# Row normalization streamed through four buffers: from tiles of 12 rows to tiles of 13, 13, 13 and 12 rows

## The chip, the cores and the metric

The kernel runs on one core of a Trainium2 chip. The metric is the device time of one execution in microseconds (us), given as the median of five runs. The profiled execution is one further run, recorded by the hardware profiler.

## The reference

```python
# x: (32, 512, 1024) float32
sums = np.sum(np.abs(x), axis=-1, keepdims=True)
return (x / (sums + 1e-8)).astype(np.float32)
```

Each of the 32 x 512 = 16384 rows of 1024 numbers is divided by the sum of its absolute values. The input is 67.11 MB, and the output is as large.

## The kernel before

The 16384 rows are spread over 128 partitions, so each partition handles 128 rows of 4 KiB. They go through in tiles. A tile holds `R = 12` rows for each partition, 48 KiB a partition and 6.29 MB in all; ten such tiles and one of 8 rows make up the 128 (`rows`, L31 to L33). In memory each tile is one contiguous block, of which partition p owns the p-th run of 12 rows (`piece`, L35 to L37).

The buffers come from one pool with `BUFS = 4` buffers of 12 rows (L39): 192 KiB a partition. Small pools of four buffers hold the sums `s` and their reciprocals `inv` (L40).

The loop over the tiles (L70) issues for each tile, in this order:

- L72, from SyncE's queue (SP): the load of the tile. Before the fifth tile and each later one SP waits until the store of the tile four places earlier has landed, since both use the same buffer.
- L45, VectorE (DVE): one reduce that gives the sum of absolute values for every row of the tile; L52 adds the epsilon, L54 takes the reciprocal.
- L55, VectorE: multiplies the first `kv = k // 2` rows of the tile by their reciprocals, in place.
- L62, ScalarE (ACT): multiplies the other `k - kv` rows, one activation for each row, in place. It runs beside L55.
- L74, from ScalarE's queue: the store of the tile. It waits for L55 and for the last activation.

The order of each queue is the order in which the loop writes its instructions (`manual_schedule`); nothing reorders them. GpSimd (POOL) only sets four constants at the start, and TensorE isn't used. Loads and stores therefore lie in two queues, q1 (issued by SP) and q10 (issued by ACT), which are served by the same 16 DMA engines.

Of the kernel before, what the change touches and what calls it, by code (L numbers as in the profile page):

```python
# [1 line left out]

# [4 lines left out]

FP32 = mybir.dt.float32
EPS = 1e-8


@with_exitstack
def kernel(
    ctx: ExitStack,
    tc: tile.TileContext,
    x: bass.AP,
    out: bass.AP,
):
    nc = tc.nc
    P = nc.NUM_PARTITIONS  # L20

    x_flat = x.flatten_outer_dims()
    out_flat = out.flatten_outer_dims()
    n, d = x_flat.shape


    R = 12
    BUFS = 4
    per_partition = n // P
    assert n % P == 0  # L30
    rows = [R] * (per_partition // R)  # L31
    if per_partition % R:
        rows.append(per_partition % R)  # L33

    def piece(flat, i):  # L35
        a, k = P * sum(rows[:i]), rows[i]
        return flat[a : a + P * k, :].rearrange("(p r) d -> p r d", p=P)  # L37

    sbuf = ctx.enter_context(tc.tile_pool(name="sbuf", bufs=BUFS))  # L39
    stats = ctx.enter_context(tc.tile_pool(name="stats", bufs=4))  # L40

    def normalize(x_tile, r0, k, kv):

        s = stats.tile([P, R], FP32)
        nc.vector.tensor_reduce(  # L45
            out=s[:, :k],
            in_=x_tile[:, r0 : r0 + k, :],
            axis=mybir.AxisListType.X,
            op=mybir.AluOpType.add,
            apply_absolute_value=True,  # L50
        )
        nc.vector.tensor_scalar_add(out=s[:, :k], in0=s[:, :k], scalar1=EPS)  # L52
        inv = stats.tile([P, R], FP32)
        nc.vector.reciprocal(out=inv[:, :k], in_=s[:, :k])  # L54
        nc.vector.tensor_mul(  # L55
            out=x_tile[:, r0 : r0 + kv, :],
            in0=x_tile[:, r0 : r0 + kv, :],
            in1=inv[:, :kv].unsqueeze(2).to_broadcast([P, kv, d]),
        )
        for r in range(kv, k):  # L60
            row = x_tile[:, r0 + r, :]
            nc.scalar.activation(  # L62
                out=row,
                in_=row,
                func=mybir.ActivationFunctionType.Copy,
                scale=inv[:, r : r + 1],
            )

    with tc.manual_schedule():
        for i, k in enumerate(rows):  # L70
            x_tile = sbuf.tile([P, R, d], FP32)
            nc.sync.dma_start(out=x_tile[:, :k, :], in_=piece(x_flat, i))  # L72
            normalize(x_tile, 0, k, k // 2)
            nc.scalar.dma_start(out=piece(out_flat, i), in_=x_tile[:, :k, :])  # L74


# [1 line left out]
_INS = ['x']  # L78
_OUTS = [((32, 512, 1024), 'float32')]


# [23 lines left out]
```

## Time and profile before

| what | value |
|---|---|
| median of five runs | 317.55 us (317.2 to 318.51) |
| profiled execution, time | 317.17 us |
| profiled execution, span from first to last instruction | 315.5 us |
| bytes moved by DMA | 134.23 MB, mean 425 GB/s over the span |
| reduce L45, 12 rows | 12.95 us each |
| reduce L45, 8 rows | 8.69 us |
| multiply L55, 6 rows | 6.56 us each |
| activation L62, one row | 1.13 us each in the page's mean; six in a row take 6.34 us |
| load L72, median from issue to landing | 38.6 us |
| store L74, median from issue to landing | 53.3 us |

The span is cut by the profiler at the first and the last instruction; 1.67 us of the execution's time lie around it. Busy times are sums over an engine's instructions and leave out the issuing of DMAs. "Landing" is the moment at which the semaphore of a DMA has its full count, and the time to it includes waiting in the queue behind earlier transfers. In the windows view each row is one stretch of the span, with its length, the busy time and instruction count of VectorE, ScalarE and GpSimd, the clock column, the mean busy share of the 16 DMA engines and the rate in GB/s.

### The profile page before, as it was taken

Reading aid. Unit: us, or ns where it says so; the run is one execution under the profiler, and the core shown is the slowest. Engines: PE = TensorE matmul, PEld = TensorE weight load, DVE = VectorE, ACT = ScalarE, POOL = GpSimd, SP = SyncE. Lnnn points to the kernel's source line nnn. Section 1 sums busy time; section 2 is a strip of 40 time slices with the busy share of each in tenths; the row PEclk is TensorE's granted clock in tenths of the full one; section 3 lists DMA queues with packets and bytes.
Section 4 is the critical chain, followed back from the end, with each engine's and each line's share of the span. In section 5 each row is a group of like instructions: output and inputs, shape, how many; then the busy total and the mean of one; then the engine's idle time right before and its main releaser. Section 6 shows DMA issues by size and latency. Waiting matters only on the chain.

```text
span 315.5 us, 227 instructions
## 1 busy us (share of the span) xinstructions
DVE 212.4 (67%) x44; ACT 69.0 (22%) x65; POOL 0.2 (0%) x4
## 2 busy tenths in 40 slices
DVE  0069999999499079719944991797099449949300
ACT  0010804308007000700440070007003400611300
POOL 0000000000000000000000000000000000000000
DMA  8999999999999999999999999999999999999996
GB/s 318 467 411 436 449 349 449 411 461 424 411 474 417 405 480 417 411 474 411 424 461 411 425 461 411 442 442 411 461 430 405 467 411 453 422 455 417 417 438 274
DMA packets 3169, 134.23 MB, mean 425 GB/s; under 512 B 352, under 2 KB 352, under 8 KB 352
## 3 DMA queue, kind: packets, MB, share of 16 engines
q1 hardware_dynamic: 1584, 67.11, 49.8%
q10 hardware_dynamic: 1584, 67.11, 49.1%
q14 instruction: 1, 0.01, 0.0%
HBM read 67.11 MB, written 67.11 MB: 425 GB/s over the span
## 4 chain that ended last, share of the span: by engine, by line
another core or an unknown queue 45%; DMA 30%; DVE 17%; SPq 1%; issue 0%; DVEq 0%; ACTq 0%
DMA x_tile<-in_x_dram 16%; DMA out_dram<-x_tile 14%; DVE s L45 11%; DVE x_tile L55 6%; SPq L72 1%; DVE inv L54 0%; DVE s L52 0%; DVEq L54 0%; ACTq L74 0%
## 5 line engine op out<-in xcount | busy, mean ns | idle before, releaser
L45 DVE TENSOR_REDUCE s<-x_tile 128x12 f32<-128x12288 f32 (+1 forms) x11 | 138.2, 12564 | 80.9 <-DMA x_tile<-in_x_dram 80.9
L62 ACT ACTIVATE x_tile<-x_tile,inv 128x1024 f32<-128x1024 f32 x64 | 67.7, 1135 | 207.4 <-DVE inv L54 207.4
L55 DVE TENSOR_TENSOR x_tile<-x_tile,inv 128x6144 f32<-128x6144 f32 (+1 forms) x11 | 70.0, 6364 | 0.4
L62 ACT ACT_TABLE_LOAD x1 | 1.3, 1283 | 18.4 <-DMA x_tile<-in_x_dram 18.4
L54 DVE RECIPROCAL inv<-s 128x12 f32<-128x12 f32 (+1 forms) x11 | 2.5, 225 | 0.9
L52 DVE TENSOR_SCALAR s<-s 128x12 f32<-128x12 f32 (+1 forms) x11 | 1.9, 173 | 0.4
L89 POOL MEMSET const-bfloat16-1.0<- 128x1 bf16 x1 | 0.1, 102 | 0.0
L89 POOL MEMSET const-uint8-127<- 128x1 uint8 x1 | 0.1, 101 | 0.0
L89 POOL MEMSET const-float32-0.0<- 128x1 f32 x1 | 0.1, 99 | 0.2 <-issue 0.2
L89 POOL MEMSET const-float32-1.0<- 128x1 f32 x1 | 0.1, 98 | 0.0
## 6 DMA issues: line engine op xcount, KB each, us to landing
x_tile<-in_x_dram SPq DMA_DIRECT2D x10, 6144.0 KB, 38.6
out_dram<-x_tile ACTq DMA_DIRECT2D x10, 6144.0 KB, 53.3
x_tile<-in_x_dram SPq DMA_DIRECT2D x1, 4096.0 KB, 33.8
out_dram<-x_tile ACTq DMA_DIRECT2D x1, 4096.0 KB, 19.5
```

The lines of the kernel that those rows point to most:

```text
L45: nc.vector.tensor_reduce(out=s[:, :k], in_=x_tile[:, r0 : r0 + k, :], axis=mybir.AxisListType.X, op=mybir.AluOpType.add, apply_absolute_v ...
L52: nc.vector.tensor_scalar_add(out=s[:, :k], in0=s[:, :k], scalar1=EPS)
L54: nc.vector.reciprocal(out=inv[:, :k], in_=s[:, :k])
L55: nc.vector.tensor_mul(out=x_tile[:, r0 : r0 + kv, :], in0=x_tile[:, r0 : r0 + kv, :], in1=inv[:, :kv].unsqueeze(2).to_broadcast([P, kv, d]),)
L62: nc.scalar.activation(out=row, in_=row, func=mybir.ActivationFunctionType.Copy, scale=inv[:, r : r + 1],)
L72: nc.sync.dma_start(out=x_tile[:, :k, :], in_=piece(x_flat, i))
L89: nc = _bacc.Bacc("TRN2", target_bir_lowering=False, num_devices=1)
```

## The change

The tile size becomes 13 rows, except in the fourth buffer, which has 12. The single pool of four equal buffers is replaced by four pools of one buffer each: 13 + 13 + 13 + 12 = 51 rows, 204 KiB a partition. The list of tiles becomes 13, 13, 13, 12, 13, 13, 13, 12, 13, 13: ten tiles for eleven.

The mapping of tiles to memory changes as well. Four tiles in a row, which fill all buffers once, form a group. The group is one contiguous block of 128 x 51 rows, of which each partition owns 51 rows in a row; tile 0 of the group takes the first 13 rows of each partition's 51, tile 1 the next 13, and so on. Within a tile a partition's 13 rows are contiguous (52 KiB), but the runs of neighbouring partitions lie 51 rows (204 KiB) apart. The third group has two tiles, 26 rows a partition.

The arithmetic, the split between VectorE (`k // 2` rows) and ScalarE (the rest) and the order of the loop stay as they are. A tile of 13 rows gives VectorE 6 rows and ScalarE 7.

```diff
-    R = 12
-    BUFS = 4
-    per_partition = n // P
+    R = 13
+    SLOTS = [R, R, R, R - 1]
     assert n % P == 0
-    rows = [R] * (per_partition // R)
-    if per_partition % R:
-        rows.append(per_partition % R)
+    left = n // P
+    rows = []
+    while left:
+        rows.append(min(left, SLOTS[len(rows) % len(SLOTS)]))
+        left -= rows[-1]
 
     def piece(flat, i):
-        a, k = P * sum(rows[:i]), rows[i]
-        return flat[a : a + P * k, :].rearrange("(p r) d -> p r d", p=P)
+        g = i - i % len(SLOTS)
+        group = rows[g : g + len(SLOTS)]
+        a, m = P * sum(rows[:g]), sum(group)
+        b = sum(rows[g:i])
+        whole = flat[a : a + P * m, :].rearrange("(p r) d -> p r d", p=P)
+        return whole[:, b : b + rows[i], :]
 
-    sbuf = ctx.enter_context(tc.tile_pool(name="sbuf", bufs=BUFS))
+    slots = [
+        ctx.enter_context(tc.tile_pool(name=f"slot{b}", bufs=1))
+        for b in range(len(SLOTS))
+    ]
...
         for i, k in enumerate(rows):
-            x_tile = sbuf.tile([P, R, d], FP32)
+            x_tile = slots[i % len(SLOTS)].tile([P, SLOTS[i % len(SLOTS)], d], FP32)
```

## The prediction

> **What bounds the kernel now.** I read the page's busy times first, then the DMA rows, then the chain of waits, the windows and the timeline.
>
> ```profile
> DVE 212.4 (67%) x44; ACT 69.0 (22%) x65; POOL 0.2 (0%) x4
> ...
> DMA  8999999999999999999999999999999999999996
> ```
> No engine is busy throughout: VectorE works two thirds of the span. The DMA row is at 9 in all slices but the first and the last, so transfers are the suspect.
>
> ```profile
> q1 hardware_dynamic: 1584, 67.11, 49.8%
> q10 hardware_dynamic: 1584, 67.11, 49.1%
> ```
> Loads (q1) and stores (q10) together take 98.9% of the time of the 16 DMA engines. 1584 packets over 11 tiles are 144 a tile: 128, one for each partition, and 16 small ones (of the 3169 packets 352, or 16 for each of the 22 DMAs, are under 512 B). So a partition's 12 rows, 48 KiB, go as one packet.
>
> ```profile
> 102.43 0.33 SPq L72
> 102.76 0.05 issue
> 102.81 0.02 SPq L72
> 102.83 28.48 another core or an unknown queue
> 131.31 0.02 issue
> 131.32 0.03 SPq L72
> 131.35 0.03 issue
> 131.38 0.33 SPq L72
> 131.71 28.64 another core or an unknown queue
> ```
> The chain runs through the loads of L72, 29.0 us apart (102.43, 131.38). Between two of them SP waits until a store has landed and so freed a buffer. In one period a tile is read and a tile is written: 2 x 6.291 MB in 29.0 us is 434 GB/s.
>
> ```profile
> 0.00:1.00 1.00, 0.00 (x0) 0.00 (x0) 0.20 (x4) 1.00 0.00 0
> 1.00:18.30 17.30, 0.00 (x0) 0.00 (x0) 0.00 (x0) 1.00 0.99 409
> 18.30:40.00 21.70, 21.55 (x5) 7.62 (x7) 0.00 (x0) 1.00 1.01 435
> 102.00:131.00 29.00, 19.83 (x5) 6.27 (x7) 0.00 (x0) 1.00 1.00 434
> ...
> 281.00:295.00 14.00, 13.48 (x4) 4.27 (x4) 0.00 (x0) 1.00 1.02 442
> 295.00:314.50 19.50, 0.00 (x0) 0.00 (x0) 0.00 (x0) 1.00 0.88 381
> ```
> The last two columns are DMA share and GB/s. The rate is the same with loads alone (18.3 to 40, 435), both (434) and stores alone (281 to 295, 442). The DMA engines themselves are the bound, and what goes through them doesn't matter. 134.22 MB at 434 GB/s are 309.3 us of the span's 315.5; the other **6.2 us** lie at the two ends (nothing before 1.0, 409 until 18.3, 381 at the end).
>
> **The change, part by part.** The reference point is the profiled execution: span 315.5, time 317.17, so 1.67 us lie around the span. The median of the five runs is 317.55, 0.38 above it.
>
> *Bytes.* The same 134.22 MB: 0.
>
> *Fewer DMAs.* 10 tiles (13, 13, 13, 12, 13, 13, 13, 12, 13, 13) for 11, so 20 DMAs for 22, 16 x 20 small packets for 352. They cost only what the DMA engines lose at a border between DMAs. From below nothing. From above: 102 to 131 holds one border of each queue, 18.3 to 40 one of a single queue, and the rates differ by under 1%, so at most 0.3 us for two borders. Between them I take the trace's single packets, which the views only sum up: one of 48 KiB takes 1.815 us, one of 32 KiB 1.213 us. That is 37.6 ns for each KiB and 9 ns fixed. Each engine moves 8 packets a DMA, so 2 x 8 x 9 ns = 0.14 us are saved in the packets; with something for the two borders, whose bound was 0.3, I take **-0.2 us**. The Trainium skill, "DMA: Bandwidth & Descriptors", section "Anatomy of one DMA", gives a DMA about 2 us of fixed cost (for the GpSimd path); were it on the path here, two fewer would give -4 us, but the window of 29 us, with two DMA ends and no loss in it, says that it is covered.
>
> *Larger pieces on the engines.* A reduce of 13 rows takes 12.95 + (12.95 - 8.69)/4 = 14.02 us. VectorE multiplies 6 rows as before (6.56), and ScalarE has 7 rows for 6: 7 x 1.057 = 7.40. From landing to store issue: 14.02 + 0.58 (the two small operations, 270.01 to 270.59) + 7.40 + 0.1 = 22.1 us, for 20.2 before. VectorE needs 14.02 + 0.58 + 6.56 = 21.2 us of a period of 2 x 6.816 MB / 434 = 31.4 us: 67% as before. Cost in mid-kernel 0, hidden by the store before, which is in its queue meanwhile.
>
> *The start.* The first tile lands 0.52 MB / 434 = 1.2 us later and its store is issued at 18.3 + 1.2 + 22.1 = 41.6 us instead of 38.4. The four loads in front hold 51 rows (26.7 MB, 61.6 us) and keep the DMA engines at work past that: 0. Each load still waits for the store four tiles back; SP has nothing else behind that wait, and POOL issues no DMA.
>
> *The tail.* This is where a larger piece could cost. Before, the last tile has 8 rows, now 13. After the last load has landed only stores can keep the DMA engines busy until the last store is issued.
>
> ```profile
> 247.43 0.33 SPq L72 DMA_DIRECT2D x_tile<-in_x_dram  x1
> 248.24 0.34 ACTq L74 DMA_DIRECT2D out_dram<-x_tile  x1
> 257.06 12.95 DVE L45 TENSOR_REDUCE s<-x_tile 128x12 f32<-128x12288 f32 x1 [8.91 <-DMA x_tile<-in_x_dram]
> ...
> 277.24 0.34 ACTq L74 DMA_DIRECT2D out_dram<-x_tile  x1
> 281.26 8.69 DVE L45 TENSOR_REDUCE s<-x_tile 128x8 f32<-128x8192 f32 x1 [4.11 <-DMA x_tile<-in_x_dram]
> ...
> 295.00 0.34 ACTq L74 DMA_DIRECT2D out_dram<-x_tile  x1
> ```
> Before: from 281 on, 442 x 14 + 381 x 19.5 = 13.6 MB are written, 4.2 of them the last tile. The 9.4 MB of older stores last 21.7 us, and the last store is issued after 13.7: 8 us to spare. After: the model is tile 9, a full one that lands at 257.06. Store 6 had landed at 247.4 (load 10 starts on it), and store 8 is queued at 248.24. In the 9.6 us between, half of the 4.2 MB moved was store 7's, so 12.58 - 2.09 = 10.5 MB are left. Scaled to 13 rows 11.4 MB, less 0.5 since tile 7 has 12 rows: 10.9 MB, **25.1 us** of cover. Needed: 22.1 us and the way from an issue to its first bytes (SP's first issue is at 0.73, the first bytes in the row from 1.0 to 2.0: at most 1.3): **23.4 us**. The cover holds with 1.7 us to spare: 0. Without it the end moves by the missing piece, microsecond for microsecond.
>
> *Addresses.* A partition's rows lie 204 KiB apart in memory (104 KiB in the last group of 26 rows) where they were 48 KiB (32 in the last tile) apart. No row shows such a pitch. Bounds: from the rows of 48 and 32 KiB, the same rate, 0 (a gain isn't excluded, but only the start could give it, below); from the start, where all engines begin at once, 17.3 us at 409 instead of 434 lose 1.0 us, and if each of the 10 loads lost that, +10 us. I take 0: within a packet the bytes are in a row as before, and both pitches known go at full rate. The Trainium skill, the same page, section "Latency and other measured facts", speaks against long pitches: copies of 16 KiB pieces at a row pitch of 512 KiB, 2 MiB and 4 MiB went at 207, 164 and 103 GB/s per direction, and 4 KiB of padding restored 214. As an estimate a loss like that at 512 KiB, 3%, would be +10 us, but 204 KiB is 51 x 4 KiB and no large power of two; no run here shows it yet.
>
> **Sum:** 315.5 - 0.2 = 315.3 us of span, 317.0 of time, and **317.4 us** as a median.
>
> **Rivals.**
> 1. *Cover gone at the tail (slower).* The engines run dry before the last store. For: only 1.7 us to spare, out of a landing time scaled by hand. Against: 25.1 comes from an observed backlog. If the last load lands so late that 3.2 us are missing from the cover, 1.5 us show: 317.4 + 1.5 = 318.9. It decides by the bound from 2.7 us less cover.
> 2. *The pitch slows packets (slower).* Place: the first packets of each jump to a new group. For: nothing in the trace has such a pitch. Against: single-direction and mixed rates are alike, so memory isn't what limits. Three groups at the 1.0 us lost at the start: 317.4 + 3 = 320.4; it decides once a 29 us window falls below 432.7 GB/s (0.3%).
> 3. *The change doesn't keep a packet a partition (slower).* With rows no longer in a row across partitions, a DMA could go row by row, 4 KiB each: 2 x 128 x 8 = 2048 packets an engine for 176, 1872 more at 9 ns = +17 us, 334. Against: the last tile fills 8 of 12 rows of its buffer, strided in SBUF, and still goes as 128 packets; the strided memory side isn't in the trace.
> 4. *The ends shrink (faster).* 6.2 us lie there. The 1.0 us of the slow start might go if other addresses let the engines begin unhindered: 316.4. Against: nothing in the change starts earlier, and the last store grows from 4.2 to 6.8 MB.
>
> **Chances.** No change that shows (forecast) 0.68; rival 1 0.07; rival 2 0.14; rival 3 0.04; rival 4 0.07. This kernel's measurement can tell about 0.3%, 0.95 us, from no change. So faster 0.07, within 0.68, slower 0.25. Range 316.5 to 319.6: the forecast's own case is 316.6 to 318.5 (the bound on each side); upward it takes in rival 1, and the small end of rival 2, which leaves out the rest of 2 and all of 3; downward it takes in some of rival 4. That leaves some 0.18 outside.
>
> **What would show it.** Right: q1 and q10 with 1440 packets each; mid-kernel windows at 434 GB/s; loads of L72 31.4 us apart; reduces of 14.0 us; 7 activations for each full tile; DMA at 9 in every inner slice; last store issued 22.1 us after the last load landed, while the DMA share is still 1.0. Wrong: a window without DMA between the last load and the last store's bytes (rival 1), windows below 432 (rival 2), thousands of packets (rival 3), or a span under 314.5 (rival 4).

## The result, and the profile after

The changed kernel takes 318.18 us (median of 29 runs, 317.44 to 319.51), the kernel before 317.54 us (median of 51 runs). The ratio is 1.0022, with an interval from 1.0016 to 1.0028: 0.64 us slower. That lies within the 0.3% that the forecast called no change and within its range, but the sign is wrong: 0.2 us less were forecast.

Every run also lists its span. The profiled execution of the changed kernel is the fastest of its 29 runs, with a span of 315.5 us as before, so the loss must be looked for in the runs:

| | time | span, median | time minus span |
|---|---|---|---|
| before, 29 runs beside the first experiments | 317.56 | 315.9 | 1.63 (1.57 to 1.68) |
| after, 29 runs | 318.18 | 316.3 | 1.91 (1.86 to 1.97) |

Two parts, then: **0.28 us outside the span**, in every run, and about **0.4 us inside** it, with more scatter (315.5 to 317.6). Medians of parts don't add up exactly, and spans are listed to 0.1 us.

Busy times, the DMA row and the queues on the page after:

```profile
DVE 207.6 (66%) x40; ACT 73.0 (23%) x69; POOL 0.2 (0%) x4
...
DMA  8999999999999999999999999999999999999995
...
q1 hardware_dynamic: 1440, 67.11, 49.8%
q10 hardware_dynamic: 1440, 67.11, 49.1%
```
The picture is the one of before: DMA engines full, VectorE at two thirds. 1440 packets a queue for 1584 are 144 for each of ten tiles, so a partition's rows still go as one packet.

Windows after (same columns as before):

```profile
1.00:18.30 17.30, 0.00 (x0) 0.00 (x0) 0.00 (x0) 1.00 0.99 409
18.30:40.00 21.70, 20.84 (x4) 7.68 (x8) 0.00 (x0) 1.00 1.01 439
102.00:133.40 31.40, 19.93 (x3) 5.64 (x6) 0.00 (x0) 1.00 1.00 434
...
296.00:314.50 18.50, 0.00 (x0) 0.01 (x1) 0.00 (x0) 1.00 0.86 374
```
The start and the middle run at the old rates, 409 and 434 GB/s, although the pieces lie 204 KiB apart.

The chain of waits after, the stretch that answers to the one shown of before:

```profile
139.14 0.33 SPq L83
139.47 29.70 another core or an unknown queue
169.18 0.02 issue
169.19 0.02 SPq L83
...
169.30 42.03 DMA x_tile<-in_x_dram
```
It runs through SP's loads as before, now 30.2 us apart here (139.14 to 169.30) and 30.9 on average from the load at 107.5 to the one at 231.1, for the 31.4 of two 13-row transfers worked out; a period with a tile of 12 rows in it is shorter.

The timeline after, with the first store and the tail:

```profile
41.02 0.38 ACTq L85 DMA_DIRECT2D out_dram<-x_tile  x1
...
265.06 0.34 ACTq L85 DMA_DIRECT2D out_dram<-x_tile  x1
274.02 14.02 DVE L56 TENSOR_REDUCE s<-x_tile 128x13 f32<-128x13312 f32 x1 [9.82 <-DMA x_tile<-in_x_dram]
...
296.04 0.34 ACTq L85 DMA_DIRECT2D out_dram<-x_tile  x1
```
From the landing of the last load to the issue of the last store it is 296.04 - 274.02 = 22.0 us, as worked out (22.1).

What no view sums up is each packet's own record. Packets can be put in a row for each of the 16 DMA engines, since one begins where the last one ends. A packet of 52 KiB takes 1.966 us and one of 48 KiB 1.815, nearly always; what a packet takes beyond that is called a hold-up below. All numbers on single DMA engines come from this reading. The mean end of the 16 engines is 313.42 us before and 313.28 after. That is 0.14 us earlier, as much as the forecast saved in packets, but two profiles of one kernel differ by as much or more (313.57 in again12, 313.79 in again13). The program waits for the last engine, which ends at 314.1 in both of these profiles.

### The profile page after: what moved, and what is told of

The parts are those of the page before. It is cut to its first block, busy times and chain, and to the rows that moved or that the text cites. A ratio compares the mean times of both kernels' runs of the same rounds, so it can differ in the third digit from the quotient of the medians.

```text
span 315.5 us, 219 instructions
## 1 busy us (share of the span) xinstructions
DVE 207.6 (66%) x40; ACT 73.0 (23%) x69; POOL 0.2 (0%) x4
## 3 DMA queue, kind: packets, MB, share of 16 engines
q1 hardware_dynamic: 1440, 67.11, 49.8%
q10 hardware_dynamic: 1440, 67.11, 49.1%
## 4 chain that ended last, share of the span: by engine, by line
DVE 33%; DMA 33%; another core or an unknown queue 21%; ACT 6%; issue 0%; SPq 0%; DVEq 0%
DMA x_tile<-in_x_dram 33%; DVE s L56 26%; ACT x_tile L73 6%; DVE x_tile L66 6%; DVE inv L65 0%; DVE s L63 0%; SPq L83 0%; DVEq L65 0%
## 5 line engine op out<-in xcount | busy, mean ns | idle before, releaser
L56 DVE TENSOR_REDUCE s<-x_tile 128x13 f32<-128x13312 f32 (+1 forms) x10 | 138.1, 13806 | 86.1 <-DMA x_tile<-in_x_dram 86.1
L73 ACT ACTIVATE x_tile<-x_tile,inv 128x1024 f32<-128x1024 f32 x68 | 71.8, 1135 | 203.9 <-DVE inv L65 203.9
L66 DVE TENSOR_TENSOR x_tile<-x_tile,inv 128x6144 f32<-128x6144 f32 x10 | 65.6, 6558 | 0.3
L65 DVE RECIPROCAL inv<-s 128x13 f32<-128x13 f32 (+1 forms) x10 | 2.4, 238 | 0.8
L63 DVE TENSOR_SCALAR s<-s 128x13 f32<-128x13 f32 (+1 forms) x10 | 1.7, 175 | 0.3
```

What stands on the lines that cost most here:

```text
L56: nc.vector.tensor_reduce(out=s[:, :k], in_=x_tile[:, r0 : r0 + k, :], axis=mybir.AxisListType.X, op=mybir.AluOpType.add, apply_absolute_v ...
L66: nc.vector.tensor_mul(out=x_tile[:, r0 : r0 + kv, :], in0=x_tile[:, r0 : r0 + kv, :], in1=inv[:, :kv].unsqueeze(2).to_broadcast([P, kv, d]),)
L73: nc.scalar.activation(out=row, in_=row, func=mybir.ActivationFunctionType.Copy, scale=inv[:, r : r + 1],)
```

## The experiments

Three theories stood at the start. T: the cover at the tail fails, so that the DMA engines wait for the last store. A, in later runs S: the addresses (A) or single hold-ups (S) make one DMA engine late, and it sets the end. O: the part outside the span has to do with the program, not with the transfers. Ratios are to the kernel before, measured beside.

**again12**: the kernel before, unchanged.

> The kernel before, unchanged, run as one of the set: a null. Every theory expects a ratio of 1.000 to the kernel before (317.5 us). It gives the span of each run beside its time, which the times of before don't show: the profiled execution of before had 1.63 us around its span, that of after 1.93. If the difference of some 0.3 us outside the span belongs to the change, the runs here show 1.6 to 1.7; if it is the recording, 1.9.

317.60 us, ratio 1.0005 (0.9989 to 1.0021), outside the span 1.64. The 0.28 us belong to the change.

**size13 and size13_b**: the new sizes, each tile contiguous again.

```diff
 def piece(flat, i):          # kernel after, with the body of before
-    ...
-    return whole[:, b : b + rows[i], :]
+    a, k = P * sum(rows[:i]), rows[i]
+    return flat[a : a + P * k, :].rearrange("(p r) d -> p r d", p=P)
```

> Tiles of 13, 13, 13 and 12 rows as after the change, but each tile a contiguous block of memory again, as before it. Theory A (addresses: the first packet of each DMA engine is slowed when the partitions' pieces lie 204 KiB apart) expects 317.4 us, and first packets like before's (about 0.8 us over the usual 1.97). Theory T (tail: the cover of 25.1 us over the needed 23.4 is so thin that it fails in part of the runs) expects 318.2 with the spread of after, from 317.4 to 319.5.

> Tiles of 13, 13, 13, 12 rows in contiguous blocks once more, for a second profile and more runs. Theory S expects a span of 316.2 again, and in the packets of its slowest DMA engine hold-ups of 0.5 us or more between 50 us and the last load, where the two profiles of the kernel before had 0.02 us. If the sizes as such cost nothing, the span is 315.9 and the first profile was chance.

318.12 and 318.08 us, ratios 1.0015 (1.0005 to 1.0026) and 1.0024 (1.0012 to 1.0035); span 316.2 both times, outside 1.91. The sizes alone bring a loss as large, in both parts. Theory A as stated falls: the first packets are held up by 0.68 us on average here, 0.79 before and 0.80 after.

**group12 and group12_b**: the new layout, with tiles of 12 rows.

```diff
 def piece(flat, i):          # kernel before
-    a, k = P * sum(rows[:i]), rows[i]
-    return flat[a : a + P * k, :].rearrange("(p r) d -> p r d", p=P)
+    g = i - i % BUFS
+    group = rows[g : g + BUFS]
+    a, m = P * sum(rows[:g]), sum(group)
+    b = sum(rows[g:i])
+    whole = flat[a : a + P * m, :].rearrange("(p r) d -> p r d", p=P)
+    return whole[:, b : b + rows[i], :]
```

> Tiles of 12 rows as before, but four tiles form one block in which each partition owns 48 rows in a row, so its pieces lie 192 KiB apart (128 KiB in the last group). Theory A (addresses) expects the slowdown here: 318.1 to 318.3 us, with first packets some 0.6 us longer than before's. Theory T (tail) expects 317.5, as the tiles and so the cover at the end are those of before.

> Tiles of 12 rows, four of them a block in which a partition owns 48 rows in a row, once more. The layout alone, by the first 12 runs: span 315.65, from 314.9 to 319.3. Theory S, with the layout as one of its causes, expects the same wide spread and a median within 0.3 of before's 315.9; one theory of the layout as a loss of its own expects 316.2 or more.

First 317.31 us (316.53 to 320.89), ratio 1.0000 (0.9976 to 1.0025); then 316.92 (316.54 to 317.44), ratio 0.9980 (0.9971 to 0.9989). The layout alone costs nothing. In the second set it gains 0.2%, and its best spans, 314.9, lie below any of before's. So there is a version that was faster than both kernels in one of two sets and no slower in the other.

**split8_5**: after, with the last tile of 13 rows as one of 8 and one of 5.

```diff
-        rows.append(min(left, SLOTS[len(rows) % len(SLOTS)]))
+        rows.append(8 if left == 13 else min(left, SLOTS[len(rows) % len(SLOTS)]))
```

> The kernel after with its last tile of 13 rows split into one of 8 and one of 5; all else as after. The last reduce takes 5.5 us instead of 14.0, and the last store is 2.6 MB instead of 6.8. Theory T (tail) expects 317.5 us with before's narrow spread, since the cover is then ample. Theory A (addresses) expects no change from after: 318.2 us.

321.19 us, ratio 1.0099 (1.0076 to 1.0122). Both theories missed it. Eleven DMA engines end between 312.9 and 313.9 us, three near 315.1, and two at 317.2 and 318.3: these two were held up by 4 to 5 us in mid-kernel, on loads and stores from 76 us on, more than half of it after 258. None waited for the last store. One late engine is enough. The part outside the span is 1.63 us here: with its last tile split, this kernel has eleven tiles, though still tiles of 13 rows.

**tail_halves**: after, with the arithmetic and the store of the last tile in two parts.

```diff
-            normalize(x_tile, 0, k, k // 2)
-            nc.scalar.dma_start(out=piece(out_flat, i), in_=x_tile[:, :k, :])
+            parts = [(0, 7), (7, 6)] if i == len(rows) - 1 else [(0, k)]
+            for r0, m in parts:
+                normalize(x_tile, r0, m, m // 2)
+                nc.scalar.dma_start(
+                    out=piece(out_flat, i)[:, r0 : r0 + m, :],
+                    in_=x_tile[:, r0 : r0 + m, :],
+                )
```

> The kernel after, with the arithmetic and the store of the last tile in two parts (7 rows, then 6); all loads and addresses as after. The first part of the last store can be issued some 12 us after the landing instead of 22. Theory T (the thin cover at the tail costs the time inside the span): the span's median falls from 316.3 to about 315.9, the one of before. Theory S (single DMA engines are held up on some packets in mid-kernel, and the slowest engine sets the end): no change, 316.3. Theory O (0.28 us lie outside the span, by how the program's instructions fall): nothing said of the span; with 12 instructions more than after the part outside may fall from 1.91 to 1.63.

318.44 us, ratio 1.0030 (1.0018 to 1.0042), span 316.45. Its timeline shows the first half stored early:

```profile
274.83 7.62 DVE L56 TENSOR_REDUCE s<-x_tile 128x7 f32<-128x7168 f32 x1 [9.87 <-DMA x_tile<-in_x_dram]
...
287.29 0.34 ACTq L87 DMA_DIRECT2D out_dram<-x_tile  x1
...
296.80 0.34 ACTq L87 DMA_DIRECT2D out_dram<-x_tile  x1
```
At 287.29 stores of older tiles are still queued, and no DMA engine waits in the tail. The span doesn't fall: 14 engines end by 313.8, two at 314.8 and 315.0. So the wait at the tail, theory T, isn't what sets the changed kernel's time.

**tail_plus2 and before_plus2**: 2.3 us more in the chain that ends with the last store, in the kernel after and in the one before.

```diff
+            if i == len(rows) - 1:
+                extra = scratch.tile([P, 2], FP32)
+                nc.vector.tensor_reduce(out=extra[:, :2], in_=x_tile[:, 0:2, :], ...)
             normalize(x_tile, 0, k, k // 2)
```

> The kernel after, with the reduce of two rows of the last tile done once more, which puts some 2.3 us into the chain that ends with the last store. Theory T with the cover already used up expects the span to grow by nearly all of it, 316.3 to 318.2 or more. With the 1.7 us to spare that the prediction worked out it grows by some 0.6. Theory S, in which the slowest engine has more left to do than the others and hides it, expects under 0.5.

> The kernel before, with the reduce of two rows of its last tile done once more, some 2.3 us in the chain that ends with the last store. The cover of before was worked out to have 8 us to spare, so the span stays at 315.9; after the change the same edit cost 1.4 us (316.3 to 317.7). If it costs here too, the cover isn't what decides.

After: 319.73 us, ratio 1.0066 (1.0053 to 1.0079), span 317.7. That is 1.4 us more, between the 0.6 and the 1.9 that theory T gave with and without the 1.7 us to spare. Timeline and windows of this run:

```profile
274.99 2.29 DVE L87 TENSOR_REDUCE extra<-x_tile 128x2 f32<-128x2048 f32 x1 [9.86 <-DMA x_tile<-in_x_dram]
...
299.20 0.34 ACTq L95 DMA_DIRECT2D out_dram<-x_tile  x1
```
```profile
296.00:298.00 2.00, 2.00 (x1) 2.00 (x3) 0.00 (x0) 1.00 0.25 107
298.00:299.00 1.00, 0.35 (x1) 1.00 (x2) 0.00 (x0) 1.00 0.00 0
299.00:300.00 1.00, 0.00 (x0) 0.17 (x1) 0.00 (x0) 1.00 0.00 0
300.00:301.00 1.00, 0.00 (x0) 0.00 (x0) 0.00 (x0) 1.00 2.00 852
```
A window counts a packet where it starts. From 298 to 300 none starts, and at 300 all 16 engines start together (852 KB in 1 us are 16 packets of 52 KiB). They waited 0.7 to 3.3 us and end together, at 315.8 to 316.0. Now the cover decides. That 2.3 us in the chain became only 1.4 in the span fits a last engine that ended about 1 us after the waiting ones without the edit (again13 below). Before: 318.06 us, ratio 1.0014 (1.0005 to 1.0023), span 316.3, some 0.4 more than the 315.85 measured beside it, where none was expected. No engine waits for the last store there. In its profile 0.2 us lie between the last packet's end and the span's end (1.6 for the usual 1.4), and the engine that ends last began at 3.90 us, later than in the other profiles of this kernel (3.5 and 3.7), and was held up by 0.7 us in mid-kernel. Whether the added reduce has to do with that is open.

**first8**: the kernel before with its tile of 8 rows first.

```diff
-        rows.append(per_partition % R)
+        rows.insert(0, per_partition % R)
```

> The kernel before, with its tile of 8 rows first and ten tiles of 12 behind it: the last tile is a full one, sizes, addresses and number of instructions otherwise as before. Cover by the prediction's way 24.2 us, needed 21.5. Theory T (a full last tile costs) expects a span of 316.1 to 316.4 for the 315.9 of before. Theory S (the 13 rows or their pitch hold engines up) expects 315.9. Outside the span 1.63 by theory O.

324.74 us, ratio 1.0217 (1.0187 to 1.0248), far beyond both theories. Its timeline and windows:

```profile
287.30 12.95 DVE L45 TENSOR_REDUCE s<-x_tile 128x12 f32<-128x12288 f32 x1 [9.26 <-DMA x_tile<-in_x_dram]
...
307.47 0.34 ACTq L74 DMA_DIRECT2D out_dram<-x_tile  x1
```
```profile
290.00:300.00 10.00, 10.00 (x1) 0.00 (x0) 0.00 (x0) 1.00 0.93 403
300.00:308.00 8.00, 7.21 (x4) 6.34 (x6) 0.00 (x0) 1.00 0.01 6
308.00:309.00 1.00, 0.00 (x0) 0.00 (x0) 0.00 (x0) 1.00 1.85 786
```
From 300 to 308 the DMA engines stand nearly still, since the last store isn't issued before 307.47. The older stores lasted 12.3 to 16.0 us beyond the landing, 13.0 on average, not the 24.2 that the prediction's way gives. The order of the packets on one DMA engine says why (L a load's packet, s a store's; the middle left out):

```
before  22 L  sLsLssLsLsLsLsLL ... LLsLsL  22 s   (8 of them the last store)
after   22 L  sLsLssLsLsLsLsLL ... LLsLsL  22 s   (8 of them the last store)
first8  18 L  sLsLsLsLsLsLssLL ... sLsLsL  18 s   (8 of them the last store)
```
From the first store on, loads and stores take turns, so the lead that the loads have gained by then comes back at the end as stores that are left. With a small first tile the first store is issued at 26.7 instead of 38.4 us, the lead is 18 packets (19 on about half of the engines) for 22 (23 on a few), and the cover 10 packets for 14: 7.3 us less. In addition the last load's semaphores come in over 5.5 us, because a late engine lands last (2.5 us before).

**pool8 and loads11**: after, with eight memsets that nothing waits for; after, with the first load as two DMAs.

```diff
+        extra = scratch.tile([P, 8], FP32)
+        for c in range(8):
+            nc.gpsimd.memset(extra[:, c : c + 1], 0.0)
```
```diff
-            nc.sync.dma_start(out=x_tile[:, :k, :], in_=piece(x_flat, i))
+            parts = [(0, 7), (7, 13)] if i == 0 else [(0, k)]
+            for r0, r1 in parts:
+                nc.sync.dma_start(out=x_tile[:, r0:r1, :], in_=piece(x_flat, i)[:, r0:r1, :])
```

> The kernel after, with eight small memsets on GpSimd at its start, which nothing waits for: 227 instructions, as many as before, for 219. Theory O, if the number of instructions in the program as a whole decides: outside the span 1.63 us instead of 1.91. If it is where the instructions of another engine end: 1.91 still. Inside the span no theory expects a change from after, 316.3; it is a second sample of after's span.

> The kernel after, with its first load issued as two DMAs (7 and 6 rows of each partition), so 11 loads in SP's queue as before; all else as after. Theory O, if SP's instructions decide: outside the span 1.63 us instead of 1.91, so 0.28 less in time at the same span. If ScalarE's or VectorE's instructions decide: 1.91. Inside the span: 316.3 by every theory.

Outside the span 1.91 and 2.08 us; span 316.65 and 316.35. Neither the number of instructions nor SP's eleven loads bring back 1.63.

**ten12**: before, without its last tile.

```diff
-    if per_partition % R:
-        rows.append(per_partition % R)
```

> The kernel before without its last tile: 120 of the 128 rows of each partition, ten tiles of 12; the rest of the output is not written. Theory O, if ten tiles instead of eleven decide: 1.91 us outside the span; if the 13 rows decide: 1.63. Span: 8.39 MB less at 434 GB/s are 19.3 us, 296.6 if the cover (24.2 us for 21.5) holds at the end of a kernel with a full last tile of 12 rows; up to 2 us more if it fails as in the kernel with the 8 rows first.

298.35 us; span 296.4, outside the span 1.92. The 0.28 us come with ten tiles, not with 13 rows; split8_5, with tiles of 13 rows but eleven tiles, has 1.63. And a full last tile of 12 rows doesn't run dry when the loads have their lead of 22 packets.

**own128**: before, with each partition owning 128 rows in a row.

```diff
-        a, k = P * sum(rows[:i]), rows[i]
-        return flat[a : a + P * k, :].rearrange("(p r) d -> p r d", p=P)
+        whole = flat.rearrange("(p r) d -> p r d", p=P)
+        return whole[:, sum(rows[:i]) : sum(rows[: i + 1]), :]
```

> The kernel before with the layout taken to its end: each partition owns 128 rows in a row, 512 KiB, so the pieces of neighbouring partitions lie 512 KiB apart; tiles of 12 rows and one of 8 as before. If the pitch slows packets as in rival 2, by the row of the Trainium skill for 512 KiB (some 3%): 327 us. If the pitch only matters for which engines are held up: 317 to 319, with spread.

323.17 us, ratio 1.0162 (1.0131 to 1.0194). Its windows:

```profile
1.00:18.30 17.30, 0.13 (x1) 0.08 (x1) 0.00 (x0) 1.00 0.99 409
18.30:40.00 21.70, 21.60 (x5) 7.55 (x7) 0.00 (x0) 1.00 1.00 435
40.00:102.00 62.00, 52.98 (x12) 14.48 (x14) 0.00 (x0) 1.00 1.00 412
...
131.00:160.00 29.00, 19.59 (x5) 6.02 (x7) 0.00 (x0) 1.00 1.00 434
160.00:189.00 29.00, 19.63 (x5) 6.06 (x7) 0.00 (x0) 1.00 1.00 427
```
Loads alone keep 435 GB/s; where loads and stores mix, some stretches fall behind. Engines were held up by 3.1 us on average in mid-kernel, for 0.1 before. So a pitch of 512 KiB does cost here; whether that comes of its length or of the power of two, no run separates. The rule that the prediction quoted from the Trainium skill ("DMA: Bandwidth & Descriptors", section "Latency and other measured facts", 207 GB/s for 214 at 512 KiB, 3%) has the right direction; this kernel lost 1.6%. At 192 and 204 KiB the rates of the windows show nothing of it.

**size13_halves and again13**: the contiguous sizes with the last tile in two parts (edit as in tail_halves), and the kernel after once more.

> Contiguous tiles of 13, 13, 13, 12 rows, with the arithmetic and the store of the last tile in two parts (7 rows, then 6). Theory T for the sizes: the 0.3 us that size13 loses inside the span (316.2 for before's 315.9) are the DMA engines' wait for the last store, 0.1 to 0.8 us in its two profiles; then the span falls to 315.9 or below. Theory S: the engine that ends last had no such wait in either profile, and was held up by 0.6 to 0.9 us in mid-kernel instead; then the span stays at 316.2.

> The kernel after, unchanged, for a second profile of it beside these runs: the first one on record was the fastest of its 29 runs (span 315.5). Theory S expects a span of 316.3 with one or two DMA engines that end 1 us or more after the others, held up in mid-kernel by 1 us or more. Theory T expects that all 16 end together after a wait of 0.3 to 1 us.

size13_halves: 317.95 us, ratio 1.0015 (1.0006 to 1.0024), span 316.0: between the two theories, 0.2 below size13 and 0.15 above the 315.85 of before beside it. again13: 318.18 us, ratio 1.0026 (1.0015 to 1.0037), span 316.3 (its profile 316.5), a typical run, and it shows both theories at once. In its timeline the last tile has landed at 274.97, and its store is issued at 296.99:

```profile
274.97 14.02 DVE L56 TENSOR_REDUCE s<-x_tile 128x13 f32<-128x13312 f32 x1 [10.00 <-DMA x_tile<-in_x_dram]
...
296.99 0.34 ACTq L85 DMA_DIRECT2D out_dram<-x_tile  x1
```
By the packets, the older stores run out 22.1 to 24.4 us after that landing, 22.6 on average over the 16 engines, and the last store's first bytes start 22.9 us after it. Thirteen engines wait 0.1 to 0.9 us for the last store, and they and one that didn't wait end within 313.6 to 313.8. Two others never wait: one ends at 314.2, one at 315.1, after 2.1 us of hold-ups in mid-kernel. The span follows this last one.

Below stand the engines of nine profiles side by side, in us. "Begin" is the start of the first packet plus its hold-up; "mid" is all hold-ups after 50 us. Hold-ups are counted against 1.966 and 1.815 us, by which they come out up to 0.1 us lower than the figures that the expectations of size13_b and size13_halves name.

```
             rows, layout       mean mid | engine that ends last: begin, mid | its end less the mean end
before       12 contiguous      0.08     | 3.48  0.00                        | 0.72
again12      12 contiguous      0.12     | 3.65  0.00                        | 0.90
size13       13 contiguous      0.14     | 3.54  0.54                        | 1.23
size13_b     13 contiguous      0.19     | 3.37  0.80                        | 1.27
group12      12 in groups       0.09     | 2.48  1.18                        | 1.20
group12_b    12 in groups       0.08     | 2.62  0.88                        | 1.09
after        13 in groups       0.22     | 2.83  0.72                        | 0.85
again13      13 in groups       0.30     | 2.76  2.05                        | 1.28
pool8        13 in groups       0.51     | 2.91  2.34                        | 1.29
```
In the contiguous kernel of 12 rows the last engine is last because its first packet came late (the mean begin is 2.6 to 2.8 in all nine). In groups no engine of these profiles begins later than 3.2, but the one that ends last has been held up in mid-kernel. On average over the engines, hold-ups are clearly larger only where both changes meet: 0.22 to 0.51 us with 13 rows in groups, 0.08 to 0.19 elsewhere. Five more profiles agree: ten12 and before_plus2 (12 contiguous) have 0.04 and 0.07 us, size13_halves (13 contiguous) 0.07, loads11 and tail_halves (13 in groups) 0.33 and 0.39.

## Why the prediction was right or wrong

The forecast was 0.2 us less, and 0.64 us more were measured. Two things that it put at nothing were not: the time around the span (0.28 us) and the end of the span (about 0.4 us), which follows the last DMA engine and not the mean rate.

*What bounds the kernel.* Right: the DMA engines do, at 434 GB/s in mid-kernel before and after. Incomplete: it treated 16 engines as one rate and the 6.2 us at the two ends as fixed. The end is that of the last engine, 0.7 to 1.3 us after the mean in the table above, and this spread moves with a change that leaves the rate alone.

*Fewer DMAs, -0.2 us.* The saving in packets was right in size and didn't count. A packet of 52 KiB takes 1.966 us (1.815 + 4 x 0.0376 = 1.965 worked out), which saves the 0.14 us; for the part above that, put down to borders between DMAs, no row shows anything. What the step leaves out is the last engine.

*Time around the span.* This is the first step that failed, and the clearest: 1.67 us (1.63 by the runs, since the span in that difference was rounded) were carried over as a constant. They became 1.91, which is 0.28 of the 0.64 us by the medians of the runs. ten12 and split8_5 tie this to ten tiles instead of eleven; one added instruction or DMA moved it too (1.77 in before_plus2, 2.08 in loads11). What happens in that time no profile here shows, so why ten tiles take longer there is open.

*Larger pieces.* Right in each number: reduce 14.02, from landing to issue 22.0 for 22.1, first store at 41.0 for 41.6.

*The tail.* The second step that failed: the cover was mis-sized. 25.1 us for 23.4 needed, so 1.7 to spare, took the 16 engines to be in step. A load lands when the slowest engine has done its part, while the fast ones are further on in the stores that are the cover. In again13 the cover was 22.6 us on average (22.1 to 24.4) for 22.9 needed, and thirteen engines had 0.1 to 0.9 us too little; in the profiled execution of after, the fastest of its runs, it was 23.0 to 24.4 for 23.1, and one engine waited, 0.1 us. Yet rival 1's mechanism doesn't set the end of the changed kernel: in after, again13, pool8 and loads11 the engine that ends last doesn't wait, and in tail_halves, where none waits, the span is 316.45. With 2.3 us more it does set it (tail_plus2). The kernel was that close.

*Addresses.* Zero was right for the rate and for the layout as a change: group12 loses nothing. But the step looked for slower packets everywhere, and the layout shows on single engines: they begin closer together, and the one that ends last was held up by about 1 us later on (0.00 us in before and again12, but 0.7 in before_plus2), with a mean over the engines that is no larger.

*The rest of the loss.* size13 loses 0.3 us of span without the layout. Taking away its wait at the tail gives 0.2 back, within a scatter of about that size. In the changed kernel taking the wait away gives nothing back (tail_halves). There the engine that ends last has been held up in mid-kernel, by 0.7 to 2.3 us in the table, and the hold-ups are larger on average than with either change alone. That the gain of the layout at 12 rows (up to 0.6 us) doesn't come with 13 rows fits this, but no run separates it, and why packets of 13 rows in groups meet more hold-ups is open.

*Rivals.* 3 fell (1440 packets a queue), and 2 too at 204 KiB (434 GB/s). 4, the ends that shrink, was half true: in groups the start does get more even, and group12 had runs of 316.5, below every run of before (the lowest is 317.01).

## What to carry to other kernels

When the DMA engines are the bound, stop counting bytes once they are all busy: the remaining tenths of a per cent belong to the engine that finishes last, and are read from how far apart the engines end, not from the mean rate. The lead that loads have when the first store starts is the cover at the end. A small first tile shortens it (here 7 us lost), a small last tile makes it last, and before a last tile is made larger, the cover has to be counted in the packets left after the last load, less the time between the first and the last engine's landing (in again13 the engines' last load packets end from 270.4 to 272.8, and the landing is at 274.97). Compare time and span run by run before explaining a small difference by the trace: nearly half of this one lay outside it.

## What the runs showed of the hardware that was not expected

- When the first store begins behind the running loads, each DMA engine has one to three load packets that together take 0.6 to 1.8 us longer, in every profile of tiles of 12 and 13 rows with pitches up to 204 KiB. It doesn't come again at that size on all engines.
- Splitting the last tile into 8 and 5 rows cost 1.0%, although from the last landing to the last store's issue it takes 9.3 us (293.06 to 302.33) instead of 22.0: two of 16 engines lost 4 to 5 us in hold-ups.
- With the tile of 8 rows first, all engines were held up in mid-kernel, 1.8 us on average for 0.1 with the same tile last. The sizes are the same; the turn in which loads and stores meet differs, and where in memory each tile begins. That reads and writes get in each other's way by their relative place is a guess that wasn't tested.
- Tiles of 13 rows in groups had hold-ups of 0.22 to 0.51 us on average in mid-kernel; the larger tiles alone and the groups alone had 0.07 to 0.19.
- Time outside the span ranged from 1.63 to 2.12 us among these kernels and was steady to about 0.05 us either way in most of them.
